# Forming three of four weight sums by adding transfers in a seven-product FFN on one Trainium2 core

## The chip, the cores and the metric

The kernel runs on one core of one Trainium2 chip. The metric is the device time of one execution in microseconds (us), all stages included. Everything is in float32, and every matrix product is made of three passes of TensorE over pairs of rounded parts (below).

## The reference, cut to what matters

Two layers of a diffusion backbone over 640 tokens (512 latent, 128 context). Each layer has an FFN, a token mixer and a second FFN, so there are four FFNs, and these are nearly all of the time:

```
def _swiglu(h, w1, w2):
    gate, up = jnp.split(h @ w1, 2, axis=-1)
    return (jax.nn.silu(gate) * up) @ w2
...
        xp = _half_ffn(xp, m_ctx, 0, norm_pre[i, 0], norm_post[i, 0], ffn_w1[i, 0], ffn_w2[i, 0])
        xs = _half_ffn(xs, m_lat, 0, norm_pre[i, 0], norm_post[i, 0], ffn_w1[i, 0], ffn_w2[i, 0])
```

D_MODEL is 1024, D_FF is 2816, that is 22 f tiles of 128 hidden channels each. For an f tile, `w1` holds a gate block and an up block of 1024 x 128.

## The kernel before, in words

**Products.** A weight tile is 128 x 1024 floats (512 KB) and is called a unit. It is loaded into a `raw` buffer (4 buffers), then split: ScalarE (ACT) writes the rounded part `hi` (line 215), VectorE (DVE) the rest `lo` (line 216); `hi` and `lo` have 6 buffers each (`wts`). TensorE (PE) then makes hi*hi, hi*lo and lo*hi (`mm3`, lines 228 to 230), each matmul with 320 moving columns, half of the tokens.

**Seven block products.** For f tiles 4 to 21 of each FFN (`FAST`) the four block products of the gate and up weights with the two halves of the tokens are made by a scheme of the Strassen-Winograd kind: seven products of 12 matmuls instead of eight. It needs four sums of weight blocks. With g1, g2 the two halves (512 columns each) of the tile's gate unit and u1, u2 those of its up unit, `send` forms g1+u1 (line 179), u1+u2 (line 180, into the up buffer), g1+u1+u2 (line 181) and -(g1+u1+u2)-g2 (line 188, into the gate buffer), all on DVE, 128 x 512 each. The four units of a tile are called `gate`, `sums`, `up` and `all`: the gate unit as loaded, the tile with g1+u1 and g1+u1+u2, the up buffer, and the half formed last. The last two f tiles (`LATE`) make the second token half later, have five products here and, instead of `up` and `all`, a unit `u2`, behind which line 197 forms the last sum for `mix`.

**Order of one f tile** (`w1_fast`): product 1 with `gate`, 2 and 3 with `sums`, 4 with `up`, 5 with `gate`, 6 with `up`, 7 with `all`. The results are taken from PSUM by ACT (lines 687, 698) and DVE (lines 690, 693, 713, 701, 719); PSUM has four `main` and two `score` banks, which go round, so that product 4 of a tile writes the bank that line 701 of the tile before has read.

**Order of the work.** `unit(i, ahead)` sends (loads, sums, splits) all units up to i+ahead when unit i is asked for; that fixes the order in which a scheduler sees them. Each engine and each DMA queue works its own list in order; `high_priority` puts the PSUM work ahead. The sums of a tile stand on DVE some one to two tiles ahead of their product. A `raw` buffer is handed on in the order of release: after line 188 the buffer of a tile's sums takes the up load of the next tile, after the split of the `all` half the buffer of its gate unit takes a later gate load.

**Stages of an FFN** (`plan_ffn`): f tiles 0 to 3 with eight products each, then f4, then a stretch of the second matrix (`w2`, some 28 us of PE), f5 to f8, `w2`, f9 to f12, `w2`, f13 to f16, `w2`, f17 to f21, and the last `w2`. A *run* below is the f tiles between two such stretches: three runs of four tiles, and one of five whose last two are `LATE`. Under the `w2` stretches DVE also makes dot products for the modulation vectors (line 421, 128 loads of 512 KB, most of them in the first three FFNs), with the same `raw` buffers.

**GpSimd (POOL)** has little to do: the power -0.5 of the norms (line 507) and small pieces of the attention.

Of the kernel before, what the change touches and what calls it, by code (L numbers as in the profile page):

```python
# [15 lines left out]
ALU = mybir.AluOpType  # L16
# [94 lines left out]
class Kernel:  # L111
# [54 lines left out]
    def send(self, kind, src):  # L166

        nc, two, one = self.nc, slice(512, UNIT), slice(0, 512)
        at = slice(0, UNIT)
        if kind in ("plain", "block", "gate"):
            raw = self.raw_tile(src)
            self.fast["gate"] = raw
        elif kind == "sums":
            up, gate = self.raw_tile(src), self.fast["gate"]
            raw = self.raw.tile([P, UNIT], F32, tag="raw", name=self.name("sums"))
            nc.vector.tensor_tensor(raw[:, one], gate[:, one], up[:, one], op=ALU.add)
            nc.vector.tensor_tensor(up[:, one], up[:, one], up[:, two], op=ALU.add)  # L180
            nc.vector.tensor_tensor(raw[:, two], gate[:, one], up[:, one], op=ALU.add)  # L181
            self.fast["up"], self.fast["sums"] = up, raw
        elif kind in ("up", "u2"):
            raw = self.fast["up"]
            at = at if kind == "up" else two
        else:
            raw, at = self.fast["gate"], two
            nc.vector.scalar_tensor_tensor(out=raw[:, two], in0=self.fast["sums"][:, two], scalar=-1.0,
                                           in1=raw[:, two], op0=ALU.mult, op1=ALU.subtract)
        n = at.stop - at.start  # L190
        if kind == "block":
            hi, lo = (self.ring(F32R)[:, :n] for _ in range(2))
        else:
            hi, lo = (self.wts.tile([P, UNIT], F32R, tag=tag, name=self.name(tag))[:, :n] for tag in ("hi", "lo"))
        self.split(hi, lo, raw[:, at])
        if kind == "u2":
            nc.vector.scalar_tensor_tensor(out=raw[:, two], in0=self.fast["sums"][:, two], scalar=-1.0,
                                           in1=self.fast["gate"][:, two], op0=ALU.mult, op1=ALU.subtract)
            self.mixed.append(raw)
        return hi, lo  # L200

# [400 lines left out]
    def ffn(self, layer, which, base, boundary):  # L602


        nc = self.nc
        n = layer * 3 + 2 * which
        begun = [False, False]
        g, sums, kept, mixes = {}, {}, {}, {}
        quad = lambda t: t.rearrange("p (c t) -> p c t", c=4)

        def hidden(f, v, half):
            lo, hi = SPAN[half]
            self.hid = self.split(g[f][:, 0, lo:hi], g[f][:, 1, lo:hi], v[:, :HALF])
# [29 lines left out]
        def part(i, k):  # L643
            return sums[i][0][:, k, :], sums[i][1][:, k, :]

        def combine(step):

            if step == 0:
                if n:
                    self.spilled = [self.dram.tile([P, 2 * TOK], F32, tag=f"spill{c}", name=self.name("spill"))  # L650
                                    for c in range(NCH // 2)]
                    for c in range(NCH // 2):
                        nc.sync.dma_start(out=self.spilled[c], in_=self.xs[n][c].rearrange("p c t -> p (c t)"))
                combine.now = {}
            k = step % 2 * 2
            b11, b12, b21, b22 = (self.pair(self.y, c, half) for c in (k, 4 + k) for half in (0, 1))
            if step < 2:
                t = combine.now[k] = [self.temp(("square", "total")[step]).rearrange("p (c t) -> p c t", c=2)
                                      for _ in range(2)]
                steps = ((1, t[0], b12, b11), (2, t[1], b22, t[0]))  # L660
            else:
                t = combine.now[k]
                steps = ((3, t[0], b22, b12), (4, t[1], t[1], b21))
            for i, to, a, b in steps:
                if k == 0:
                    sums[i] = [quad(self.ring(F32R)) for _ in range(2)]
                nc.vector.tensor_tensor(to, a, b, op=ALU.subtract)
                self.split(sums[i][0][:, k : k + 2, :], sums[i][1][:, k : k + 2, :], to)

        high, tt = self.tc.high_priority, nc.vector.tensor_tensor  # L670

        def product(f, ps, unit, at, x, start):
            w = mixes[f] if unit is None else self.unit(base + self.w1_at[f] + unit)
            for k in range(4):
                a = at + k * P
                self.mm3(ps, w[0][:, a : a + P], w[1][:, a : a + P], *x(k), start and k == 0, k == 3, not start)
# [32 lines left out]
        def one(f, a, unit):  # L709
            w = self.bank()[:, :HALF]  # L710
            product(f, w, unit, 0, lambda k: part(1, k), True)
            with high():
                tt(a, a, w, op=ALU.add)
            return w

        def two(f, a, q, w, unit, at):
            product(f, w, unit, at, lambda k: self.h.chunk(4 + k, 1), False)
            with high():
                nc.vector.scalar_tensor_tensor(out=q, in0=w, scalar=-1.0, in1=q, op0=ALU.mult, op1=ALU.subtract)  # L719
                nc.scalar.activation(q, q, AF.Silu)  # L720
                tt(a, a, q, op=ALU.mult)
                hidden(f, a, 1)

        def tail(f):
            a, q = kept[f]
            two(f, a, q, one(f, a, None), None, 512)
# [42 lines left out]
        for op, a, half in self.ffn_plan:  # L769
# [3 lines left out]
            if op == "w1":  # L773
                if not begun[half]:
                    self.finish(half)
                    begun[half] = True
                w1(a, half)
            elif op == "combine":
                combine(a)
            elif op == "fast":  # L780
                w1_fast(a)
            elif op == "mix":
                mixes[a] = self.mix()
            elif op == "tail":
                tail(a)
            elif op == "w2":
                w2(a[0], half, a[1])
                if a[0] < len(SLICES) - 1:
                    passed += 1
                    due = BEHIND[n] * passed // (2 * NCH * (len(SLICES) - 1))  # L790
                    self.behind(due - done)
                    done = due
            elif op == "x":
                self.new_x(n + 1)
                for c in range(NCH // 2):
                    src = self.spilled[c].rearrange("p (c t) -> p c t", c=2) if n else self.io["x"][:, 2 * c : 2 * c + 2, :]
                    nc.sync.dma_start(out=self.xs[n + 1][c], in_=src)
            else:
                boundary(half, acc[half])
# [659 lines left out]
```

## Time and profile before

| | |
|---|---|
| time, median of 3 runs | 2282.19 us (2278.74 to 2282.55) |
| profiled execution | 2277.9 us, span 2276.0 us |
| PE matmul busy | 2241.0 us, 98% of the span |
| DVE busy | 1732.3 us, 76% |
| ACT busy | 1269.3 us, 56% |
| POOL busy | 41.8 us, 2% |
| loads and stores, q1 | 274.63 MB, 36.9% of 16 engines' span |
| granted TensorE clock | 0.997 |

A row of the timeline gives start, duration, engine, line, operation, the tile written and those read, and in brackets how long the engine sat idle before it and on what. A row of the waits gives who waited for whom, the total in us, how often, and the longest. In a row of the windows each engine's busy time stands with its number of instructions. A row of the DMA issues gives the transfer, how often, its size and the median time from issue to landing.

### The profile page before, as it was taken

Reading aid. Unit: us, or ns where it says so; the run is one execution under the profiler, and the core shown is the slowest. Engines: PE = TensorE matmul, PEld = TensorE weight load, DVE = VectorE, ACT = ScalarE, POOL = GpSimd, SP = SyncE. Lnnn points to the kernel's source line nnn. Section 1 sums busy time; section 2 is a strip of 40 time slices with the busy share of each in tenths; the row PEclk is TensorE's granted clock in tenths of the full one; section 3 lists DMA queues with packets and bytes.
Section 4 is the critical chain, followed back from the end, with each engine's and each line's share of the span. In section 5 each row is a group of like instructions: output and inputs, shape, how many; then the busy total and the mean of one; then the engine's idle time right before and its main releaser. Section 6 shows DMA issues by size and latency. Waiting matters only on the chain.

```text
span 2276.0 us, 39329 instructions
## 1 busy us (share of the span) xinstructions
PE 2241.0 (98%) x15680; PEld 2208.5 (97%) x15680; DVE 1732.3 (76%) x3014; ACT 1269.3 (56%) x2460; POOL 41.8 (2%) x64
## 2 busy tenths in 40 slices
PE   7999999999999999999999999999999999999998
PEld 5999999999999999999999999998998999999998
DVE  5889888588788888868878888588677485766674
ACT  4445554565654555556545544577778654545545
POOL 0000000000000000000000000000000000000000
PEclk9999999999999999999999999999999999999999
DMA  8244443334333433443244443424333222332322
GB/s 316 90 133 154 161 130 115 145 97 129 113 112 112 148 120 123 136 160 112 86 128 141 157 130 103 148 92 136 119 111 102 82 72 98 112 93 78 104 88 102
DMA packets 80281, 278.14 MB, mean 122 GB/s; under 512 B 8800, under 2 KB 15200, under 8 KB 79968
## 3 DMA queue, kind: packets, MB, share of 16 engines
q1 hardware_dynamic: 79280, 274.63, 36.9%
q8 instruction: 123, 2.02, 0.4%
q10 hardware_dynamic: 816, 0.98, 0.1%
q14 instruction: 62, 0.51, 0.1%
HBM read 264.04 MB, written 11.53 MB: 121 GB/s over the span
## 4 chain that ended last, share of the span: by engine, by line
PE 92%; DVE 3%; ACT 2%; DMA 2%; issue 0%; DVEq 0%; POOL 0%; SPq 0%; ACTq 0%
PE main L228 27%; PE main L230 26%; PE main L229 26%; PE score L230 3%; PE score L229 3%; PE score L228 3%; PE sum L1286 1%; DMA raw<-in_qkv 1%; DVE lo L216 1%; PE sum L512 1%; PE sum L502 1%; PE score L1219 1%; DMA first<-in_w_mod_k 1%; DVE ring L1065 1%; DVE ring L1077 0%
## 5 line engine op out<-in xcount | busy, mean ns | idle before, releaser
L228 PE MATMUL main<-ring,hi 128*128 128x320 f32 x3872 | 1205.3, 312 | 1.6 <-ACT ring L215 1.6
L229 PE MATMUL main<-ring,hi 128*128 128x320 f32 x3872 | 1197.9, 309 | 1.0 <-DVE ring L216 1.0
L230 PE MATMUL main<-ring,lo 128*128 128x320 f32 x3872 | 1197.4, 309 | 0.0
L228 PEld LDWEIGHTS main<-ring,hi 128*128 128x128 f32 x3872 | 727.8, 188 | 6.2 <-issue 2.7
L229 PEld LDWEIGHTS main<-ring,hi 128*128 128x128 f32 x3872 | 727.9, 188 | 2.0 <-DVE ring L216 1.4
L230 PEld LDWEIGHTS main<-ring,lo 128*128 128x128 f32 x3872 | 727.5, 188 | 0.2 <-issue 0.2
L215 ACT ACTIVATE hi<-raw 128x1024 fp32r<-128x1024 f32 (+1 forms) x366 | 356.1, 974 | 443.5 <-PE main L229 353.6
L216 DVE TENSOR_TENSOR lo<-raw,hi 128x1024 fp32r<-128x1024 f32 (+1 forms) x366 | 408.9, 1118 | 142.2 <-ACT hi L215 140.6
L421 DVE SCALAR_TENSOR_TENSOR junk<-raw,wide 128x1024 bf16<-128x1024 f32 x256 | 312.9, 1222 | 21.0 <-DMA raw<-in_w_mod_t 18.5
L763 ACT ACTIVATE y<-main 128x320 f32<-128x320 f32 x318 | 135.9, 432 | 150.6 <-PE main L230 150.0
L737 ACT ACTIVATE main<-y 128x320 f32<-128x320 f32 x256 | 111.5, 439 | 40.2 <-DVE left L719 27.2
L230 PE MATMUL score<-ring,lo 128*128 128x320 f32 x416 | 128.7, 309 | 0.6 <-DVE lo L216 0.6
L228 PE MATMUL score<-ring,hi 128*128 128x320 f32 x416 | 128.9, 310 | 0.0
L229 PE MATMUL score<-ring,hi 128*128 128x320 f32 x416 | 128.5, 309 | 0.0
L216 DVE TENSOR_TENSOR lo<-sums,hi 128x1024 fp32r<-128x1024 f32 x72 | 88.1, 1223 | 42.6 <-ACT hi L215 42.6
L457 DVE TENSOR_TENSOR total<-total,square 128x640 f32<-128x640 f32 x71 | 58.4, 825 | 80.4 <-ACT square L456 78.6
L215 ACT ACTIVATE hi<-sums 128x1024 fp32r<-128x1024 f32 x72 | 76.3, 1060 | 31.2 <-DVE sums L181 16.8
L228 PE MATMUL main<-ring,ring 128*128 128x320 f32 x288 | 90.9, 316 | 0.0
L230 PE MATMUL main<-ring,ring 128*128 128x320 f32 x288 | 89.1, 310 | 0.0
L229 PE MATMUL main<-ring,ring 128*128 128x320 f32 x288 | 88.9, 309 | 0.0
L230 PEld LDWEIGHTS score<-ring,lo 128*128 128x128 f32 x416 | 78.1, 188 | 0.8 <-DVE lo L216 0.8
L228 PEld LDWEIGHTS score<-ring,hi 128*128 128x128 f32 x416 | 78.1, 188 | 0.0
(211 smaller groups left out, 2599.8 us busy)
## 6 DMA issues: line engine op xcount, KB each, us to landing
raw<-in_w SPq DMA_DIRECT2D x264, 512.0 KB, 3.6
raw<-in_w_mod_t SPq DMA_DIRECT2D x128, 512.0 KB, 4.2
raw<-in_qkv SPq DMA_DIRECT2D x26, 512.0 KB, 3.7
first<-in_w_mod_k SPq DMA_DIRECT2D x16, 512.0 KB, 8.7
spill<-ring SPq DMA_DIRECT2D x12, 640.0 KB, 3.6
ring<-spill SPq DMA_DIRECT2D x12, 640.0 KB, 7.0
raw<-in_bias SPq DMA_DIRECT2D x16, 448.0 KB, 3.3
raw<-in_four_in SPq DMA_DIRECT2D x8, 512.0 KB, 5.8
```

What stands on the lines that cost most here:

```text
L215: a = self.nc.scalar.activation(hi, src, AF.Copy)
L216: return a, self.nc.vector.tensor_tensor(lo, src, hi.bitcast(F32), op=ALU.subtract)
L228: mm(out, whi, xhi, start=start, stop=False)
L229: mm(out, whi, xlo, start=False, stop=False)
L230: self.latest = mm(out, wlo, xhi, start=False, stop=stop)
L421: last = self.nc.vector.scalar_tensor_tensor(out=self.junk, in0=raw, scalar=1.0, in1=self.wide[:, cond, :], op0=ALU.mult, op1=ALU.mult, ac ...
L457: nc.vector.tensor_tensor(acc, acc, sq, op=ALU.add)
L502: self.meant = nc.tensor.matmul(ps[:, j : j + 1], part[:, t : t + P], self.mean, start=i == j == 0 or len(acc) == 1, stop=i == len(acc) - ...
L512: self.spread = nc.tensor.matmul(bank[:, t : t + P], col[:, j : j + 1].to_broadcast([P, P]), self.ident, start=True, stop=True)
L737: nc.scalar.activation(ps[:, :HALF], self.y[:, m, lo:hi], AF.Copy)
L763: nc.scalar.activation(self.y[:, m, lo:hi], ps[:, :HALF], AF.Copy)
L1065: nc.vector.tensor_tensor(ks[p0][rows, KL + to : KL + to + hi - lo], ps[rows, lo - base : hi - base], ks[p0][rows, to : to + hi - lo].bitc ...
```

## The change

What `send` does for `sums` and `all` is changed: of the four sums only g1+u1+u2 is still formed on DVE.

- u1+u2: a transfer from HBM, issued by POOL, adds u2 into the up buffer (line 180 of the new kernel).
- g1+u1: the sums buffer is loaded with g1 by SP (line 179, 256 KB), and a transfer issued by POOL adds u1 to it (line 181).
- the last sum: a transfer issued by POOL adds the tile's g1+u1+u2 from its buffer into the second half of the gate buffer (line 189). A transfer only adds, so the sum has the other sign now, and the lines that use it (in `combine`, `one`, `two`) are changed to match; the instructions there keep their number and shapes.
- behind `u2`, line 197 becomes a plain addition on DVE.
- `product` asks for units four ahead instead of three.

```
             raw = self.raw_tile(src)
-            self.fast["gate"] = raw
+            self.fast["gate"], self.fast["from"] = raw, src
         elif kind == "sums":
             up, gate = self.raw_tile(src), self.fast["gate"]
             raw = self.raw.tile([P, UNIT], F32, tag="raw", name=self.name("sums"))
-            nc.vector.tensor_tensor(raw[:, one], gate[:, one], up[:, one], op=ALU.add)
-            nc.vector.tensor_tensor(up[:, one], up[:, one], up[:, two], op=ALU.add)
+            nc.sync.dma_start(out=raw[:, one], in_=self.fast["from"][:, one])
+            nc.gpsimd.dma_start(out=up[:, one], in_=src[:, two], accum_op=ALU.add)
+            nc.gpsimd.dma_start(out=raw[:, one], in_=src[:, one], accum_op=ALU.add)
             nc.vector.tensor_tensor(raw[:, two], gate[:, one], up[:, one], op=ALU.add)
...
             raw, at = self.fast["gate"], two
-            nc.vector.scalar_tensor_tensor(out=raw[:, two], in0=self.fast["sums"][:, two], scalar=-1.0,
-                                           in1=raw[:, two], op0=ALU.mult, op1=ALU.subtract)
+            nc.gpsimd.dma_start(out=raw[:, two], in_=self.fast["sums"][:, two], accum_op=ALU.add)
...
-            nc.vector.scalar_tensor_tensor(out=raw[:, two], in0=self.fast["sums"][:, two], scalar=-1.0,
-                                           in1=self.fast["gate"][:, two], op0=ALU.mult, op1=ALU.subtract)
+            nc.vector.tensor_tensor(raw[:, two], self.fast["sums"][:, two], self.fast["gate"][:, two], op=ALU.add)
...
-                steps = ((1, t[0], b12, b11), (2, t[1], b22, t[0]))
+                steps = ((1, t[0], b11, b12, ALU.subtract), (2, t[1], b22, t[0], ALU.add))
...
-            w = mixes[f] if unit is None else self.unit(base + self.w1_at[f] + unit)
+            w = mixes[f] if unit is None else self.unit(base + self.w1_at[f] + unit, 4)
...
-                tt(a, a, w, op=ALU.add)
+                tt(a, a, w, op=ALU.subtract)
...
-                nc.vector.scalar_tensor_tensor(out=q, in0=w, scalar=-1.0, in1=q, op0=ALU.mult, op1=ALU.subtract)
+                tt(q, w, q, op=ALU.subtract)
```

From line 189 on the new kernel's line numbers are one lower: the split is at 214 and 215, the PSUM reads of DVE at 689, 692, 712, 700, 718.

**DVE, in the first FFN, while PE makes f6.** `left`, `right` and `main` belong to the PSUM work of f6, `raw` and `sums` to weight buffers; the number tells buffers of one name apart. Before:

```order
L713 TENSOR_TENSOR left_1462<-left_1462,main_1519 128x320
L179 TENSOR_TENSOR sums_1654<-raw_1619,raw_1652 128x512
L180 TENSOR_TENSOR raw_1652<-raw_1652 128x512
L181 TENSOR_TENSOR sums_1654<-raw_1619,raw_1652 128x512
L216 TENSOR_TENSOR lo_1603<-raw_1487,hi_1602 128x512
L701 TENSOR_TENSOR right_1465<-left_1463,main_1468 128x320
L702 TENSOR_TENSOR right_1465<-right_1465,right_1464 128x320
L216 TENSOR_TENSOR lo_1622<-raw_1619,hi_1621 128x1024
```

And now, at the same place:

```order
L712 TENSOR_TENSOR left_1470<-left_1470,main_1533 128x320
L182 TENSOR_TENSOR sums_1631<-raw_1610,raw_1629 128x512
L215 TENSOR_TENSOR lo_1582<-raw_1477,hi_1581 128x512
L700 TENSOR_TENSOR right_1473<-left_1471,main_1476 128x320
L701 TENSOR_TENSOR right_1473<-right_1473,right_1472 128x320
L215 TENSOR_TENSOR lo_1613<-raw_1610,hi_1612 128x1024
```

Of the three sums one is left, at the same place: behind the PSUM read of product 4, ahead of the PSUM read of product 6 (line 701, now 700) and of the split of the next gate unit. It reads the up buffer `raw_1629` that a POOL transfer adds into.

**POOL, the same stretch of the program** (nothing of POOL stood between the norms there before). Its list for f7, f8 and the first tile of the next run:

```order
L180 DMA raw_1496<-in_w 128x512
L181 DMA sums_1498<-in_w 128x512
L189 DMA raw_1477<-sums_1498 128x512
L180 DMA raw_1629<-in_w 128x512
L181 DMA sums_1631<-in_w 128x512
L189 DMA raw_1610<-sums_1631 128x512
```

Three transfers for each f tile, in one list: the one into the up buffer waits for the up load, the one into the gate buffer for the sum on DVE and for the split of the gate unit, which reads what it overwrites.

More of the change, by code (lines that the diff above doesn't have):

```diff
@@ L659, in combine @@
                                       for _ in range(2)]
-                steps = ((1, t[0], b12, b11), (2, t[1], b22, t[0]))
+                steps = ((1, t[0], b11, b12, ALU.subtract), (2, t[1], b22, t[0], ALU.add))
             else:
                 t = combine.now[k]
-                steps = ((3, t[0], b22, b12), (4, t[1], t[1], b21))
-            for i, to, a, b in steps:
+                steps = ((3, t[0], b22, b12, ALU.subtract), (4, t[1], t[1], b21, ALU.subtract))
+            for i, to, a, b, op in steps:
                 if k == 0:
                     sums[i] = [quad(self.ring(F32R)) for _ in range(2)]
-                nc.vector.tensor_tensor(to, a, b, op=ALU.subtract)
+                nc.vector.tensor_tensor(to, a, b, op=op)
                 self.split(sums[i][0][:, k : k + 2, :], sums[i][1][:, k : k + 2, :], to)
```

## The prediction

> **What bounds the kernel now.** I read the page first, then the engines by stretch, then who PE waits for.
>
> ```profile
> span 2276.0 us, 39329 instructions
> PE 2241.0 (98%) x15680; PEld 2208.5 (97%) x15680; DVE 1732.3 (76%) x3014; ACT 1269.3 (56%) x2460; POOL 41.8 (2%) x64
> ```
>
> The windows of three f tiles of the second FFN and of the `w2` stretch behind them (length, then PE, weight loads, DVE, ACT, POOL, clock, DMA share, GB/s):
>
> ```profile
> 728.85:741.17 12.32, 12.32 (x86) 12.32 (x85) 10.59 (x18) 5.92 (x10) 0.00 (x0) 1.00 0.27 84
> 741.17:753.49 12.32, 12.32 (x86) 12.32 (x85) 8.69 (x15) 5.92 (x10) 0.00 (x0) 1.00 0.47 146
> 765.81:793.97 28.16, 28.16 (x194) 28.16 (x193) 26.08 (x42) 16.49 (x35) 0.00 (x0) 1.00 0.47 150
> ```
>
> PE has no gap in these stretches, at full clock, while DVE is busy 10.6 of 12.3 us and 26.1 of 28.2. DVE is the second most loaded engine, but it doesn't set the pace. First PE instructions of product 2 (the only ones into `score`) of two tiles that follow each other:
>
> ```profile
> 742.93 0.31 PE L228 MATMUL score<-ring,hi 128*128 128x320 f32 x1
> 755.25 0.31 PE L228 MATMUL score<-ring,hi 128*128 128x320 f32 x1
> ```
>
> A tile takes 755.25 - 742.93 = 12.32 us for 84 matmuls, 0.1467 each, 1.76 for a product; it starts one product earlier, at 741.17. What PE waited for on DVE's splits, in the whole execution:
>
> ```profile
> PE score L229 <- DVE lo L216: 1.4, 2, 1.3
> PE main L229 <- DVE ring L216: 1.0, 1, 1.0
> PE score L230 <- DVE lo L216: 0.6, 1, 0.6
> ```
>
> That is 3.0 us in all, 0.13% of the span. So the bound is PE's own rate, and a lighter DVE can't bring more than about 3 us here.
>
> **What the change removes.** Duration of each group: least, median, most, in ns.
>
> ```profile
> L179 DVE TENSOR_TENSOR sums<-raw,raw x72: 684/686/700, 56.0 to 2193.8; 128x512 f32<-128x512 f32 x72
> L180 DVE TENSOR_TENSOR raw<-raw x72: 684/691/698, 58.9 to 2194.8; 128x512 f32<-128x512 f32 x72
> L188 DVE SCALAR_TENSOR_TENSOR raw<-sums,raw x64: 684/691/695, 82.2 to 2172.9; 128x512 f32<-128x512 f32 x64
> ```
>
> 72 x 0.686 + 72 x 0.691 + 64 x 0.691 = 143 us of DVE, some 2.1 us of each tile. PE waits for none of it, so on the path it is worth 0, at most the 3.0 us above. The turned signs and line 197 keep their instructions: 0.
>
> **What it adds.** 72 loads of 256 KB on SP and 72 + 72 + 64 = 208 adding transfers of 256 KB on POOL's queue. DMA issues, with the median from issue to landing:
>
> ```profile
> raw<-in_w SPq DMA_DIRECT2D x264, 512.0 KB, 3.6
> first<-in_w_mod_k SPq DMA_DIRECT2D x16, 512.0 KB, 8.7
> ring<-spill SPq DMA_DIRECT2D x12, 640.0 KB, 7.0
> x_out<-ring SPq DMA_DIRECT2D x7, 320.0 KB, 2.5
> k_out<-rms SPq DMA_DIRECT2D x8, 64.0 KB, 1.5
> sk<-in_conds SPq DMA_DIRECT2D x1, 8.0 KB, 2.1
> q1 hardware_dynamic: 79280, 274.63, 36.9%
> ```
>
> Bytes: 72 x 3 x 256 KB from HBM and 64 x 256 KB inside SBUF are 73 MB; at 36.9% for 274.63 MB that is 10 points more, 47% of the DMA engines. Not a bound; it lies beside PE.
>
> What counts is latency. No row shows a transfer that adds. Call A1 the time from issue to landing of the one from HBM into the up buffer, A3 of the one from the sums buffer into the gate buffer. From 8 KB in 2.1 to 512 KB in 3.6 is 1.5 us for 504 KB, so 256 KB lands in 2.85. An adding transfer has to read its destination too: 0.75 more, 3.6. I add 0.4 for an issue by software, which no row gives: A1 = 4.0. A3: 2.5 for 320 KB out of SBUF, 0.2 less for 256 KB, the second read and the issue as above: 3.4. Bounds: 2.1 and 1.5 below (the smallest transfers), 8.7 and 7.0 above (loads that queue). I take the middle since the 512 KB load moves as many bytes and is unqueued. The Trainium skill, "DMA: Bandwidth & Descriptors", section "Anatomy of one DMA — SWDGE (gpsimd) path", gives a transfer issued by GpSimd 2.0 us and its bytes over 436 GB/s, so 2.6 us for 256 KB; no row can show it, and by it the sum below comes out at nothing (first rival).
>
> **The new loop.** DVE while PE makes f6 (728.85 on) and f7 (741.17 on) of the second FFN, the place of the order above; two loads stand below:
>
> ```profile
> 736.47 0.48 DVE L713 TENSOR_TENSOR left<-left,main 128x320 f32<-128x320 f32 x1
> 736.87 0.69 DVE L179 TENSOR_TENSOR sums<-raw,raw 128x512 f32<-128x512 f32 x1
> 737.59 0.69 DVE L180 TENSOR_TENSOR raw<-raw 128x512 f32<-128x512 f32 x1
> 738.31 0.69 DVE L181 TENSOR_TENSOR sums<-raw,raw 128x512 f32<-128x512 f32 x1
> 738.92 0.69 DVE L216 TENSOR_TENSOR lo<-raw,hi 128x512 fp32r<-128x512 f32 x1
> 739.61 0.49 DVE L701 TENSOR_TENSOR right<-left,main 128x320 f32<-128x320 f32 x1
> 740.21 0.49 DVE L702 TENSOR_TENSOR right<-right,right 128x320 f32<-128x320 f32 x1
> 740.62 1.22 DVE L216 TENSOR_TENSOR lo<-raw,hi 128x1024 fp32r<-128x1024 f32 x1
> ...
> 744.09 0.69 DVE L188 SCALAR_TENSOR_TENSOR raw<-sums,raw 128x512 f32<-128x512 f32 x1
> ```
> ```profile
> 744.84 0.33 SPq L157 DMA_DIRECT2D raw<-in_w  x1
> ```
>
> Before, f8's sums are complete at 739.00, 2.2 us before f7 starts, and the up load of the next tile goes out at 744.84, when line 188 (end 744.78) has let go of the sums buffer: 3.7 us into a tile. Now that load waits for the landing of the transfer of line 189, which reads the sums buffer. Line 189 waits on POOL for the sum on DVE and for the split of the gate unit, four DVE instructions later. And the sum waits for the transfer into the up buffer. So each tile hangs on the one before: up load 3.6, A1, sum 0.7, the DVE work to the end of the gate split 740.62 + 1.22 - 738.92 = 2.9, A3, and some 0.1 at each of four handovers (an estimate): 7.6 + 4.0 + 3.4 = 15.0 us against a tile of 12.32. Within a run the sums fall back by 2.7 us per tile.
>
> How far they may fall: behind the sum on DVE stand a split (0.69) and the PSUM read of product 6 (0.49), which product 4 of the next tile waits for, 3 x 1.76 = 5.28 us into it. So the sum may end up to 5.28 - 0.69 - 0.49 = 4.1 us after that tile's start; now it ends 2.2 before. The cover is 6.3 us. Behind the sum, DVE's whole list waits, ACT's next splits with it.
>
> Within a run: the first tile's sums are formed under `w2`. For the third tile the up load goes out 3.7 us into the first, so its sum ends at 3.7 + 3.6 + A1 + 0.7 + 0.2 = 12.2, 0.1 before the second tile starts. Fourth tile: 2.6 after the third starts. Fifth: 5.3, past the limit by 1.2. Only the long run has a fifth, once in each FFN: 4 x 1.2 = 4.8 us.
>
> In the first FFN two runs start late, since the dot products on DVE (line 421) hold up the sums. Last sum of the second tile, and product 2 of the first:
>
> ```profile
> 288.61 0.31 PE L228 MATMUL score<-ring,hi 128*128 128x320 f32 x1
> 366.05 0.31 PE L228 MATMUL score<-ring,hi 128*128 128x320 f32 x1
> ```
> ```profile
> 289.58 0.69 DVE L181 TENSOR_TENSOR sums<-raw,raw 128x512 f32<-128x512 f32 x1
> 365.99 0.69 DVE L181 TENSOR_TENSOR sums<-raw,raw 128x512 f32<-128x512 f32 x1
> ```
>
> They end 3.4 us (290.27 against 286.85) and 2.4 us (366.68 against 364.29) into the run. With line 189 behind them the next up load goes out at 3.4 + 0.1 + A3 + 0.1 = 7.0 and 6.0 instead of 3.7, so the fourth tile's sum ends at 2.6 + 3.3 = 5.9 and 2.6 + 2.3 = 4.9: stalls of 1.8 and 0.8; and in the long one the fifth is 2.7 past the limit instead of 1.2. That is 1.8 + 0.8 + 1.5 = 4.1 us.
>
> Units four ahead: the `hi` split of a unit waits for a `wts` buffer that PE lets go of, which a longer list does not hasten.
>
> ```profile
> ACT hi L215 <- PE main L229: 366.2, 191, 8.1
> ```
>
> Worth 0 beside that wait; where it is short of raw buffers, SP's list only blocks earlier. Below nothing is excluded too, but for the 3.0 us.
>
> Sum: 4.8 + 4.1 = 8.9 us. The profiled execution took 2277.9 (span 2276.0), so 2286.8, say **2287 us**. That execution lies 4.3 below the median of the three runs and 0.8 below the fastest, so a median may come out some 4 higher; the range has room for it.
>
> **The rivals.** 0.2%, 4.6 us, is about what a measurement of this kernel tells from no change.
>
> *The loop fits (not slower).* If A1 + A3 is 6.9 or less, the fifth tile's sum ends within its 4.1 us, and what is left is about 3 us in the first FFN. For it: 3.5 us for the pair by the smallest rows, and landing times of loads include HBM, which the second read doesn't. Against: each of the two must beat a plain 512 KB load. Time 2278, with the median at 2282. The Trainium skill's 2.0 us and bytes over 436 GB/s, from the page named above, would put the pair at 5.2 and decide for this one; the traces bear neither out.
>
> *The transfers are far slower.* With A1 = 7.0 and A3 = 6.4 (queued loads show 8.7 and 7.0) the loop is 21.0 us, 8.7 more than a tile: third sum 2.9 into its tile, fourth 11.6, so 7.5 of stall in each short run and 7.5 + 8.7 = 16.2 in the long one, 4 x (3 x 7.5 + 16.2) = 155 us: 2433. For it: POOL must write what the transfer does while DVE is busy 76% of the span. Against: the 512 KB loads are unqueued at 3.6. At both upper bounds it is some 230 us. The Trainium skill, "SBUF — State Buffer", section "SBUF: two separate sides", tells of a transfer issued by GpSimd that took about 3100 ns beside a DVE copy instead of 620, because DVE held the port through which the descriptors are written; its section "Who interferes with whom" does not count two-input additions that meet a GpSimd write among these. No row here shows it.
>
> *Faster.* The 3.0 us of waits on splits vanish, and the lighter DVE shortens a norm or the attention. Nothing in the waits shows more than that: 2273.
>
> **How the numbers follow.** Forecast (A1 + A3 from 6.9 to 9): 0.41, of which 0.06 lands within 0.2%. The loop fits: 0.39. Far slower: 0.15. Faster: 0.05. The forecast and the fit are close, and the forecast is what the middle values give. So faster 0.05, same 0.06 + 0.39 = 0.45, slower 0.35 + 0.15 = 0.50. At A1 + A3 = 9 (4.9 and 4.1) the loop grows by 4.3 per tile: the short runs stall 1.0, the long one 5.3, 4 x 8.3 = 33, and some 9 more in the first FFN: 2320, on the scale of the median 2324. The range, 2275 to 2335, holds the forecast, the fit and half of the faster case, and leaves out most of the far slower one.
>
> **What would show it.** Right: PE without a gap in the first three tiles of a run and gaps at line 227 behind line 700 in the fifth; DVE idle ahead of line 182 for some 5 us per tile, released by the transfer of line 180; POOL's transfers landing in 3.4 to 4.0 us; DVE busy some 143 us less. The forecast is wrong if the sums of a run don't fall back from tile to tile, if PE's stalls lie under `w2` (ACT waiting for line 181 ahead of the PSUM seeds) or at the norms (line 506 behind a transfer on POOL), or if the two kinds of transfers land in under 3.4 or over 4.5 us.

## The result and the profile after

The changed kernel takes 2474.84 us (median of 4 runs, 2471.95 to 2476.53) against 2281.72 (4 runs of the kernel before beside it): 1.0848 times as long, interval 1.0829 to 1.0866. It lost 193 us where the prediction had 9 and its range ended at 2335. The profiled execution took 2476.53, with a span of 2474.8.

The page's head, for the kernel after:

```profile
span 2474.8 us, 40081 instructions
PE 2303.7 (93%) x15680; PEld 2245.0 (91%) x15680; DVE 1596.7 (65%) x2806; ACT 1253.9 (51%) x2460; POOL 224.2 (9%) x272
```

DVE is lighter by 1732.3 - 1596.7 = 135.6 us, near the 143 that were counted. PE, which had no time to lose, is now idle 7% of the span. Whom its matmuls waited for (us in all, times, longest):

```profile
PE main L227 <- ACT main L736: 45.2, 12, 6.7
PE main L227 <- DVE left L692: 39.9, 34, 3.9
PE main L227 <- ACT left L686: 38.3, 29, 4.4
```

These are reads of PSUM (lines 686, 692) and the seeding of a PSUM bank under `w2` (line 736), 123 us together. What PE lacks is mostly not weights but banks, because DVE and ACT come late to read or fill them. Why they are late stands in their own waits, after:

```profile
DVE sums L182 <- DMA raw<-in_w: 301.7, 64, 8.2
```
```profile
ACT ring L214 <- DVE right L701: 207.3, 52, 8.3
ACT hi L214 <- DMA sums<-in_w: 204.9, 35, 10.0
```

DVE stands 302 us at its sum for the landing of line 180, ACT 205 us at a split for the landing of line 181 and 207 behind DVE. The transfers themselves took what was forecast (KB each, median us from issue to landing):

```profile
sums<-in_w SPq DMA_DIRECT2D x72, 256.0 KB, 3.4
raw<-in_w POOLq DMA_DIRECT2D x72, 256.0 KB, 3.9
sums<-in_w POOLq DMA_DIRECT2D x72, 256.0 KB, 5.1
raw<-sums POOLq DMA_DIRECT2D x64, 256.0 KB, 3.3
```

A1 is 3.9 (forecast 4.0), A3 is 3.3 (forecast 3.4). Line 181, 5.1 us behind a load of 3.4, had been given no price.

**A tile.** Two tiles of the second FFN after (length, then PE, weight loads, DVE, ACT, POOL, clock, DMA share, GB/s), at the place where the tile before took 12.32 without a gap:

```profile
800.57:815.88 15.31, 13.11 (x86) 12.32 (x85) 8.57 (x14) 5.60 (x9) 1.06 (x2) 1.00 0.57 135
815.88:831.20 15.32, 13.15 (x87) 12.37 (x86) 10.65 (x18) 6.13 (x10) 2.59 (x3) 1.00 0.60 137
```

The loop of the prediction is there, at its length. DVE's sum of one tile and of the next (in brackets DVE's idle time before), POOL's issues between them, and SP's up load:

```profile
804.42 0.69 DVE L182 TENSOR_TENSOR sums<-raw,raw 128x512 f32<-128x512 f32 x1 [8.08 <-DMA raw<-in_w]
...
819.70 0.69 DVE L182 TENSOR_TENSOR sums<-raw,raw 128x512 f32<-128x512 f32 x1 [5.96 <-DMA raw<-in_w]
```
```profile
808.26 0.86 POOL L189 DMA_DIRECT2D raw<-sums  x1 [7.49 <-DVE left L718]
815.91 0.86 POOL L180 DMA_DIRECT2D raw<-in_w  x1 [6.79 <-DMA raw<-in_w]
```
```profile
811.58 0.33 SPq L157 DMA_DIRECT2D raw<-in_w  x1
```

From sum to sum 819.70 - 804.42 = 15.28 us: 3.84 to the issue of line 189, 3.3 to the up load (it goes out as that transfer lands), 4.33 to the issue of line 180, 3.79 to the next sum. Forecast: 15.0. What was wrong is how soon it hurts. ACT at that place:

```profile
806.75 0.47 ACT L214 ACTIVATE ring<-right 128x320 fp32r<-128x320 f32 x1 [6.78 <-DVE right L701]
807.12 1.04 ACT L214 ACTIVATE hi<-sums 128x1024 fp32r<-128x1024 f32 x1
808.28 0.47 ACT L719 ACTIVATE left<-left 128x320 f32<-128x320 f32 x1
808.66 0.42 ACT L686 ACTIVATE left<-main 128x320 f32<-128x320 f32 x1
```

DVE's lateness goes over to ACT, whose list holds a split of 1.04 us and two more instructions ahead of line 686. That read ends at 809.08, 8.5 us into the tile, and product 5 wanted its bank after 4 x 1.76 = 7.04. PE's waits in that tile:

```profile
PE main L227 <- DVE left L692: 1.1, 1, 1.1
PE main L227 <- ACT left L686: 0.9, 1, 0.9
PE main L227 <- DVE right L700: 0.2, 1, 0.2
```

The reads by lines 692 and 686 cost it 2.0 us; line 700, the only one that the prediction priced, 0.2. The tile is 3.0 us longer, of which 15.31 - 13.11 = 2.2 is idle time of PE; the rest counts as busy, since at a gap the modelled end of one MATMUL no longer overlaps the next.

**Under `w2`.** ACT after, in the stretch of `w2` behind the same run:

```profile
858.93 1.06 ACT L214 ACTIVATE hi<-sums 128x1024 fp32r<-128x1024 f32 x1 [5.54 <-DMA sums<-in_w]
859.89 0.42 ACT L762 ACTIVATE y<-main 128x320 f32<-128x320 f32 x1
...
861.16 0.43 ACT L736 ACTIVATE main<-y 128x320 f32<-128x320 f32 x1
```
```profile
851.75 0.87 POOL L189 DMA_DIRECT2D raw<-sums  x1 [4.18 <-ACT main L736]
852.38 1.13 POOL L181 DMA_DIRECT2D sums<-in_w  x1
```

Line 181 is issued at 852.38, behind line 189 on POOL's queue, and ACT gets on at 858.93, 6.5 us later. The seed behind it comes at 861.16, and PE waits. It is so in all twelve of PE's waits for line 736: ahead of the seed, ACT stood 3.8 to 10.0 us at the split of a sums unit for line 181. The gap shown (the last column but two is the granted clock):

```profile
859.50:861.64 2.14, 0.00 (x0) 0.00 (x0) 1.62 (x2) 2.14 (x5) 0.00 (x0) 1.00 0.00 0
861.64:866.20 4.56, 4.56 (x20) 4.56 (x21) 3.84 (x7) 3.65 (x9) 0.00 (x0) 0.63 0.83 255
```

After the gap the clock is 0.63 for 4.56 us, which costs 4.56 x 0.37 = 1.7 us on top of the 2.14.

**Where the 193 us lie.** The trace has 80 first MATMULs into `score` (one per fast tile and two more in each FFN). The profiled spans differ by 2474.8 - 2276.0 = 198.8 us. The distances between those matmuls, after less before, sum to 194.0 within the FFNs, 70.2, 44.1, 55.8 and 23.9 in the four FFNs; 122.4 of it between tiles, 71.7 in distances with `w2` in them. Only 4.8 us lie outside. For PE, 136 us of the 198.8 are more idle time (span less busy time, 171.1 against 35.0) and 2303.7 - 2241.0 = 62.7 are more busy time for the same 15680 matmuls. The lower clock behind the gaps is some 48 us of that (an estimate from the mean granted clocks: (1 - 0.978) x 2474.8 - (1 - 0.997) x 2276.0), a quarter of the loss.

### The profile page after: what moved, and what is told of

The parts are those of the page before. It is cut to its first block, busy times and chain, and to the rows that moved or that the text cites. A ratio compares the mean times of both kernels' runs of the same rounds, so it can differ in the third digit from the quotient of the medians.

```text
span 2474.8 us, 40081 instructions
## 1 busy us (share of the span) xinstructions
PE 2303.7 (93%) x15680; PEld 2245.0 (91%) x15680; DVE 1596.7 (65%) x2806; ACT 1253.9 (51%) x2460; POOL 224.2 (9%) x272
## 4 chain that ended last, share of the span: by engine, by line
PE 43%; DMA 28%; DVE 16%; issue 8%; ACT 5%; POOL 1%; DVEq 0%; POOLq 0%; SPq 0%; ACTq 0%
DMA raw<-in_w 14%; PE main L227 12%; PE main L228 12%; PE main L229 12%; DMA sums<-in_w 8%; DVE lo L215 6%; DMA raw<-in_w_mod_t 4%; ACT hi L214 2%; DVE junk L420 2%; DVE ring L215 1%; PE score L228 1%; PE score L227 1%; PE score L229 1%; ACT ring L214 1%; DMA raw<-sums 1%
## 5 line engine op out<-in xcount | busy, mean ns | idle before, releaser
L227 PE MATMUL main<-ring,hi 128*128 128x320 f32 x3872 | 1231.5, 318 | 138.5 <-ACT main L736 45.2
L228 PE MATMUL main<-ring,hi 128*128 128x320 f32 x3872 | 1212.3, 313 | 1.4 <-DVE ring L215 1.3
L229 PE MATMUL main<-ring,lo 128*128 128x320 f32 x3872 | 1210.8, 313 | 0.0
L227 PEld LDWEIGHTS main<-ring,hi 128*128 128x128 f32 x3872 | 741.1, 191 | 168.9 <-DVE left L692 49.1
L228 PEld LDWEIGHTS main<-ring,hi 128*128 128x128 f32 x3872 | 742.0, 192 | 2.7 <-DVE ring L215 2.1
L229 PEld LDWEIGHTS main<-ring,lo 128*128 128x128 f32 x3872 | 740.7, 191 | 0.2 <-issue 0.2
L182 DVE TENSOR_TENSOR sums<-raw,raw 128x512 f32<-128x512 f32 x72 | 49.9, 693 | 315.6 <-DMA raw<-in_w 301.7
L214 ACT ACTIVATE ring<-right 128x320 fp32r<-128x320 f32 x104 | 48.0, 468 | 230.5 <-DVE right L701 207.3
L180 POOL DMA_DIRECT2D raw<-in_w x72 | 63.1, 876 | 996.9 <-DMA raw<-in_w 302.2
L227 PE MATMUL main<-ring,ring 128*128 128x320 f32 x288 | 90.9, 316 | 0.0
L228 PE MATMUL main<-ring,ring 128*128 128x320 f32 x288 | 89.1, 309 | 0.0
```

Source lines behind the costliest of these rows:

```text
L180: nc.gpsimd.dma_start(out=up[:, one], in_=src[:, two], accum_op=ALU.add)
L214: a = self.nc.scalar.activation(hi, src, AF.Copy)
L227: mm(out, whi, xhi, start=start, stop=False)
L228: mm(out, whi, xlo, start=False, stop=False)
L229: self.latest = mm(out, wlo, xhi, start=False, stop=stop)
```

## The experiments

Theories. *Loop:* the tile's chain through the raw buffers is 15.3 us, and everything follows from it. *Lists:* DVE and ACT work through lists in order, a consumer of a transfer stands in them where the operand has not landed, and PSUM reads stand behind it. *Transfers:* their bytes, their issues on POOL or their own slowness. "Loss" is the median less that of the kernel before in the same call.

### One part at a time

Lines 180 and 189 back on DVE, so that only g1+u1 is a transfer:

```diff
-            nc.gpsimd.dma_start(out=up[:, one], in_=src[:, two], accum_op=ALU.add)
+            nc.vector.tensor_tensor(up[:, one], up[:, one], up[:, two], op=ALU.add)
...
-            nc.gpsimd.dma_start(out=raw[:, two], in_=self.fast["sums"][:, two], accum_op=ALU.add)
+            nc.vector.tensor_tensor(raw[:, two], self.fast["sums"][:, two], raw[:, two], op=ALU.add)
```

> Only the sum g1+u1 is formed by a transfer (lines 179 and 181); the other two are back on DVE, with the new signs. The loop theory (each up load hangs on the last sum's transfer, which hangs on DVE's sum, which hangs on the adding transfer into the up buffer: 15.3 us per tile against 12.32) expects no loss, 2282 within 5 us, since both links of the loop that are transfers are gone. The rival theory (ACT waits in order for the landing of line 181, and PSUM reads and seeds stand behind it) expects that a large part of the loss stays, 2330 to 2420, with ACT hi<-sums waiting on the transfer for over 100 us and PE behind lines 686, 692 and 736.

Only line 180 a transfer (lines 179, 181 and 189 on DVE):

> Only u1+u2 is formed by a transfer (line 180); it waits on POOL until DVE has read the up buffer for g1+u1. The loop theory: without the last sum's transfer the up load again goes out about 3.7 us into a tile, lands 3.7 later, the DVE sum takes 0.7, the issue 0.65, the transfer 3.7: the sum on DVE begins about 12.5 us in, at the start of the next tile, and does not fall back further: 2282 to 2305. The ACT theory expects 2282, as nothing that ACT waits for is a transfer of line 181.

Only line 189 a transfer:

> Only the last sum (line 189) is a transfer. The loop theory: the up load waits for it, so a tile's chain is 3.7 (load) + 2.1 (three DVE sums less the one that overlaps) + 2.9 + 0.65 + 3.3 = 12.6 us, 0.3 over a tile: 2282 to 2300. The ACT theory expects 2282.

Lines 180 and 189 transfers, g1+u1 on DVE behind line 182:

```diff
+            nc.vector.tensor_tensor(raw[:, one], raw[:, two], up[:, two], op=ALU.subtract)
```

> u1+u2 and the last sum stay transfers, g1+u1 is formed on DVE from the finished sums (g1 + (u1+u2) - u2, another rounding), so nothing waits for line 181. The loop theory: the loop stays, 0.7 us longer by the DVE instruction, so the loss stays: 2430 to 2500. The ACT theory: the loss goes, 2282 to 2310.

| as transfers | median us | ratio, 95% interval | loss us |
|---|---|---|---|
| g1+u1 | 2384.59 | 1.0435 to 1.0479 | 104.0 |
| u1+u2 | 2379.99 | 1.0418 to 1.0449 | 99.4 |
| last sum | 2287.59 | 1.0018 to 1.0042 | 7.0 |
| u1+u2 and last | 2405.26 | 1.0529 to 1.0561 | 124.6 |

Neither theory comes out as its expectation had it. With g1+u1 alone the loop through line 189 is gone, and 104 us are lost. With u1+u2 alone line 181 is gone, and 99 us are lost where both theories had at most 25. The waits of ACT in the first kernel and of DVE in the second (line 181 there is DVE's sum):

```profile
ACT hi L214 <- DMA sums<-in_w: 257.4, 62, 8.7
```
```profile
DVE sums L181 <- DMA raw<-in_w: 218.9, 66, 5.4
```

Yet neither kernel is free of a loop. The buffer of a tile's sums is let go by the split of the sums unit too, not by the last sum alone, and that split comes late in both. Two up loads of the second FFN that follow each other, with ACT's part of that split between them, in the kernel with g1+u1 alone:

```profile
928.36 0.33 SPq L157 DMA_DIRECT2D raw<-in_w  x1
940.95 1.06 ACT L214 ACTIVATE hi<-sums 128x1024 fp32r<-128x1024 f32 x1 [4.11 <-DMA sums<-in_w]
943.29 0.33 SPq L157 DMA_DIRECT2D raw<-in_w  x1
```

The two are 14.93 us apart, and the second goes out 0.03 us after DVE's part of the split has ended, at 943.26. The split had waited 4.1 us for line 181. With u1+u2 alone, two up loads at about the same place:

```profile
929.64 0.33 SPq L157 DMA_DIRECT2D raw<-in_w  x1
942.92 0.33 SPq L157 DMA_DIRECT2D raw<-in_w  x1
```

Here it is 13.28 us, still over the 12.32 of a tile; the transfer of that kernel takes 5.3 us in the median, where its expectation had 3.7. So these two kernels do not separate the waits in the lists from a loop through the raw buffers: each has both. The last sum as a transfer costs next to nothing alone: 1.6 of its 7.0 us lie in the FFNs.

### Four ahead, or fewer

All sums on DVE, four ahead kept:

> No sum is formed by a transfer: all three are back on DVE. What stays of the change is the turned signs and the units asked for four ahead. The prediction's term of 0 for both expects 2282 within 5 us. A theory that the four ahead itself moves splits in front of PSUM reads and costs time expects 2300 or more.

```diff
-            w = mixes[f] if unit is None else self.unit(base + self.w1_at[f] + unit, 4)
+            w = mixes[f] if unit is None else self.unit(base + self.w1_at[f] + unit)
```

> All of the change but the four ahead: units are asked for three ahead, so DVE's sum and the splits stand one unit later in DVE's and ACT's lists. The theory of the blocked lists (DVE stands at its sum for the landing of line 180, ACT at its split for the landing of line 181, with PSUM reads behind them, and what counts is how late in the lists they stand) expects a good part of the loss gone: each run of tiles gains one unit's time of cover, some 3 us in each of 16 runs and as much under w2: 2370 to 2430. The loop alone (15.3 us per tile, whatever the lists) expects 2455 to 2480.

> All of the change, but units are asked for two ahead, so the sum and the splits stand two units later in the lists than in the changed kernel. Blocked lists: 2310 to 2390, unless PE then waits for weights. Loop alone: 2455 to 2480.

> Lines 179 to 181 are transfers, the last sum is back on DVE (no loop), units are asked for two ahead. Blocked lists and loop together: the up load goes out about 3.7 us into a tile, lands 3.7 later, issue 0.65, transfer 3.7 to 5, so the operands are there 12 to 13 us in, and with the sum placed two units later DVE and ACT hardly wait: 2282 to 2305. If the loss came from anything else in the transfers (their bytes, POOL's issues, HBM traffic) it stays: 2380 or more.

| kernel | median us | ratio, 95% interval | loss us |
|---|---|---|---|
| no transfers, four ahead | 2286.48 | 1.0014 to 1.0037 | 5.6 |
| all, three ahead | 2474.65 | 1.0840 to 1.0872 | 193.8 |
| all, two ahead | 2477.50 | 1.0848 to 1.0891 | 196.6 |
| all but the last sum, two ahead | 2423.69 | 1.0610 to 1.0642 | 142.8 |

The four ahead and the turned signs cost nothing in the FFNs (the distances between tiles are those of before; the 5.6 us lie outside them), as forecast. My expectation for three and two ahead was wrong: nothing moved. So the last kernel, whose 2424 us falls under "2380 or more", does not speak for another cause in the transfers either: its sums did not come later, as its expectation took for granted. The order of DVE's list shows why: the framework's scheduler orders each engine's list itself. Whether units are asked for four, three or two ahead, the same 30 of the 72 sums stand ahead of a read by line 700, with no other of these reads between.

### Consumers later in the lists

So the order was forced (below, the *late* order, against the *planned* one of the kernel after): line 182 and the splits of the sums unit and of the last unit are queued behind the PSUM reads (and seeds) traced before them; three ahead.

```diff
+            with self.behind_of(*self.mark.values()):
-            nc.vector.tensor_tensor(raw[:, two], gate[:, one], up[:, one], op=ALU.add)
+                nc.vector.tensor_tensor(raw[:, two], gate[:, one], up[:, one], op=ALU.add)
...
-                nc.scalar.activation(a, x, AF.Copy)
+                self.mark["act"] = nc.scalar.activation(a, x, AF.Copy)
...
-                tt(a, q, z, op=ALU.subtract)
+                self.mark["dve"] = tt(a, q, z, op=ALU.subtract)
```

> All four transfers of the change stay; units are asked for three ahead, and DVE's sum (line 182) and the splits of the sums unit and of the last one are held in DVE's and ACT's lists behind the PSUM reads traced before them (the sum behind line 692 of the tile before, the split behind its line 686). Blocked lists (DVE and ACT stand at the consumer of a transfer that has not landed, with PSUM reads queued behind it): the loss mostly goes, 2285 to 2340, since a landing 4 us later no longer stands in front of those reads; DVE's wait at the sum falls from 302 us to under 100. Loop alone, or slowness of the transfers themselves: the sums come no faster, 2400 to 2480.

> As the kernel with the late use, but with the last sum back on DVE, so that the loop has one transfer less. Blocked lists: 2282 to 2310, a little under the kernel with all four transfers. If the loop through the last sum is what is left there, the difference between the two is that rest; if it isn't, the two are equal.

> Control: the same order of the lists as in the kernel with the late use, but all three sums on DVE and no adding transfer. It prices the order itself: 2282 to 2295 if the splits still come in time for PE; more if PE then waits for weights, which would have to be taken off the two kernels above.

> The order of the lists of the kernel with the late use, but only u1+u2 is a transfer (line 180); g1+u1 is taken on DVE from the finished sums (g1 + (u1+u2) - u2, another rounding), the last sum on DVE. Compare with only u1+u2 by a transfer in the planned order (2380). If the price is that DVE stands at its sum ahead of PSUM reads, the late order takes most of it away: 2282 to 2310. If the price is in the transfer itself (the up buffer held longer, loads behind it), it stays: 2360 to 2400.

> The late order with u1+u2 and the last sum as transfers and g1+u1 on DVE from the finished sums: the loop is whole, line 181 is gone. If what is left in the kernel with the late use (2434) is ACT's wait for line 181, this falls to 2285 to 2320. If it is the loop, it stays at 2390 to 2440.

Line 189 queued behind line 181 on POOL, in the kernel with all four transfers:

```diff
-            nc.gpsimd.dma_start(out=raw[:, one], in_=src[:, one], accum_op=ALU.add)
+            self.added = nc.gpsimd.dma_start(out=raw[:, one], in_=src[:, one], accum_op=ALU.add)
...
+            with self.behind_of(self.added):
```

> The kernel with the late use, with line 181 always ahead of line 189 of the same tile on POOL. Under w2 POOL's list has them the other way round, so line 181 waits there for DVE's sum, and ACT for line 181 with PSUM reads and seeds behind it. If that order is a large part of the rest, 2360 to 2410, with the loss under w2 halved from 85 us; if line 181 is late for its own sake, 2425 to 2440.

| transfers, late order | median us | ratio, 95% interval | loss us | loss in the planned order |
|---|---|---|---|---|
| none | 2281.19 | 0.9995 to 1.0014 | 1.1 | |
| u1+u2 | 2330.88 | 1.0196 to 1.0230 | 48.2 | 99.4 |
| u1+u2 and last | 2373.89 | 1.0387 to 1.0418 | 91.2 | 124.6 |
| all but last | 2391.55 | 1.0437 to 1.0508 | 111.5 | 142.8 |
| all | 2433.98 | 1.0662 to 1.0693 | 153.9 | 193.1 |
| all, line 181 ahead of 189 | 2441.49 | 1.0687 to 1.0719 | 158.8 | |

The order of the lists is worth 31 to 51 us in each pair, and costs nothing without transfers, so blocked lists are part of the loss. (Two pairs differ in more: "all but last" was asked for two ahead in the planned order, and "u1+u2" takes g1+u1 from the finished sums in the late order, so that its transfer need not wait for that sum, and lands in 3.8 us instead of 5.3.) They are not most of it, 39 of the 193 us for the whole change, and the expectations of 2285 to 2340 for all four, 2282 to 2310 for "all but last" and for "u1+u2", and 2285 to 2320 for "u1+u2 and last" were all too low. DVE's wait at the sum fell (line 185 is that sum here), and ACT's at the split grew:

```profile
DVE sums L185 <- DMA raw<-in_w: 85.7, 42, 5.0
```
```profile
ACT hi L218 <- DMA sums<-in_w: 336.4, 58, 10.9
```

Between tiles the loss fell from 122 to 56 us; in the distances with `w2` it rose from 72 to 85. A sum moved behind one read stands ahead of the next: 48 of the 72 now stand ahead of the read by line 717 (712 before). POOL's order of lines 181 and 189 brought nothing: with `w2` the loss fell from 85 to 73 us, between tiles it rose from 56 to 84. That leaves an earlier start of the operands, and SP's queue shows what holds their loads, in the kernel after:

```profile
SPq L157 <- DMA raw<-sums: 502.5, 55, 31.1
```

55 loads wait for the transfer of the last sum, which reads the buffer that they go to. In the kernel before, loads waited there for line 188 on DVE, 31 times and 4.9 us at most:

```profile
SPq L157 <- DVE raw L188: 135.8, 31, 4.9
```

There are four raw buffers, and a tile takes three.

### More raw buffers

`NRAW`, the number of raw buffers, 4 to 5, with `NBLK`, that of the large buffers named `ring`, 20 to 19 to make room (and 6 with 18). Without transfers, as a control:

> Control for the two kernels with five raw buffers (and 19 blocks instead of 20, to make room): all sums on DVE, three ahead. 2282 to 2300 if one block less costs little; what it costs is to be taken off the other two.

The whole change, its planned order, four ahead:

> The whole change, four ahead, with five raw buffers instead of four: up loads no longer hang on the buffer that the last sum's transfer reads, so the loop opens. If the loop through that buffer is the bulk of the loss, it goes: 2300 to 2380. If DVE and ACT stand at consumers that the planned order puts right behind the transfers wherever these are, it stays: 2420 to 2475.

> Five raw buffers and the late order together: transfers go out earlier and their consumers stand later. Blocked lists expect the loss to shrink most of all kernels with the four transfers: 2300 to 2380, with ACT's wait for line 181's transfer (336 us with four buffers) under 200. If neither lead nor order is what is missing, 2420 to 2440 as with four buffers.

> The whole change in its planned order, four ahead, with six raw buffers and 18 blocks (four buffers: 193 us lost, five: 65, of which 54 in the two FFNs that load most of the modulation weights beside the tiles). If the loss is lead that the raw buffers don't give, the rest falls again: 2282 to 2320. If the rest with five buffers is the transfers' own (their bytes, POOL's issues, the landing times themselves), it stays: 2335 to 2355. One block less may cost something of its own; with 19 blocks it cost 1.4 us.

| kernel | median us | ratio, 95% interval | loss us | of it in the four FFNs |
|---|---|---|---|---|
| no transfers, five | 2282.51 | 0.9997 to 1.0016 | 1.4 | none |
| whole change, four | 2474.84 | 1.0829 to 1.0866 | 193.1 | 70.2, 44.1, 55.8, 23.9 |
| whole change, five | 2345.81 | 1.0264 to 1.0305 | 64.7 | 26.4, 1.1, 28.0, 5.0 |
| five, late order | 2339.64 | 1.0243 to 1.0273 | 58.6 | 24.5, 7.3, 20.1, 7.7 |
| whole change, six | 2304.33 | 1.0082 to 1.0116 | 23.8 | 4.0, 1.2, 5.4, 0.5 |

One buffer takes two thirds of the loss away, in the planned order, a second most of the rest; with five the late order is worth at most some 6 us (the intervals overlap) instead of 39. A tile and the `w2` stretch of the second FFN with five buffers:

```profile
760.86:773.18 12.32, 12.32 (x86) 12.32 (x85) 8.75 (x15) 5.78 (x10) 2.60 (x3) 1.00 0.64 156
785.50:825.98 40.48, 40.48 (x278) 40.48 (x277) 32.53 (x56) 23.54 (x47) 6.12 (x7) 1.00 0.78 214
```

PE is back at 12.32 and 40.48 with the same transfers, at a higher DMA share (0.64 and 0.78 against 0.57) and with more bytes per second (156 to 214 GB/s; before, 84 to 150 in such stretches). So bytes, POOL's issues and contention are not what costs time in this FFN. In the first and the third, which keep 26.4 and 28.0 us, the sixth buffer takes away most of the rest with the same transfers, which speaks against them there too. With six buffers DVE and PE wait as follows:

```profile
DVE sums L182 <- DMA raw<-in_w: 163.2, 56, 7.4
```
```profile
PE main L227 <- DVE left L692: 8.0, 7, 1.7
```

DVE still stands 163 us at its sum, and PE loses 8 us by line 692 instead of 39.9: a wait of DVE for a transfer costs little as long as its operands come early enough against PE. Of the 2302.5 - 2276.0 = 26.5 us by which the profiled spans differ, 11.0 lie in the FFNs; 8.0 are added ahead of the fourth FFN (412.1 us between the tiles around it against 404.1), where two blocks fewer may tell; a control with six buffers wasn't run.

## Why the prediction was wrong

- **The bound, and the worth of the lighter DVE: right.** 135.6 us of DVE bought nothing: even with the loss nearly gone (six buffers, 2304.33) no kernel with the change beats the one before.
- **The sizes of the transfers and the loop: right, in part by luck.** 3.9 and 3.3 against 4.0 and 3.4; 15.28 against 15.0. The parts were not: a plain load of 256 KB took 3.4 in this kernel (2.7 with g1+u1 alone), not 2.85, so that what the adding cost over it is 0.5 and not 1.15. No run shows the 0.4 for an issue by software by itself; what the loop above shows is that POOL began the issue of line 180 0.67 us after the load had landed, where the sum had 0.1 for a handover.
- **"The cover is 6.3 us": the step that failed.** It had two ends, and both were off. The start: the prediction let the first tiles' sums be formed under `w2` at no cost, with the third tile's sum ending 0.1 before the second tile starts. In the run shown, the second tile's sum was already late:

```profile
789.51 0.69 DVE L182 TENSOR_TENSOR sums<-raw,raw 128x512 f32<-128x512 f32 x1 [4.42 <-DMA raw<-in_w]
```
```profile
790.01 0.31 PE L227 MATMUL score<-ring,hi 128*128 128x320 f32 x1
...
802.33 0.31 PE L227 MATMUL score<-ring,hi 128*128 128x320 f32 x1
```

  A tile starts 1.76 before its first MATMUL into `score`, the first tile of this run at 788.25 and the second at 800.57. So the second tile's sum ends (790.20) 2.0 us into the first tile. In the kernel before, it ended at 713.94, 2.6 ahead of the first tile (718.29 - 1.76 = 716.53):

```profile
713.25 0.69 DVE L181 TENSOR_TENSOR sums<-raw,raw 128x512 f32<-128x512 f32 x1
```
```profile
718.29 0.31 PE L228 MATMUL score<-ring,hi 128*128 128x320 f32 x1
```

  After, that is 4.6 us later, and the third tile's sum ends (805.11) 4.5 into the second, not 0.1 ahead. The limit: only line 700 for product 4 was counted, 4.1 us. Line 686 for product 5 and line 692 for product 6 stand behind more work in both lists. The fourth FFN shows it most plainly: the third tile's sum ended there at 2109.87, a microsecond ahead of the second tile (2112.67 - 1.76 = 2110.91), and PE still stalled in that tile, because ACT stood at the split that needs line 181, and DVE at its own part of that split, with line 692 behind it:

```profile
2109.18 0.69 DVE L182 TENSOR_TENSOR sums<-raw,raw 128x512 f32<-128x512 f32 x1 [2.48 <-issue]
```
```profile
2112.67 0.31 PE L227 MATMUL score<-ring,hi 128*128 128x320 f32 x1
```
```profile
2116.02 1.06 ACT L214 ACTIVATE hi<-sums 128x1024 fp32r<-128x1024 f32 x1 [4.04 <-DMA sums<-in_w]
2116.98 0.46 ACT L719 ACTIVATE left<-left 128x320 f32<-128x320 f32 x1
2117.34 0.42 ACT L686 ACTIVATE left<-main 128x320 f32<-128x320 f32 x1
```
```profile
PE main L227 <- DVE left L692: 0.9, 1, 0.9
```

  So the loss is not in the fifth tile of the long run alone: the third tile loses 1.5 to 4.5 us in each of the 16 runs, the second 0.7 to 3.1 in 15 of them, and the fourth of the long ones 5.4 to 6.5. In the first FFN, where two late starts were priced at 4.1 us, the first tile of every run loses 4.4 to 6.2 as well.
- **Line 181: left out of the sum.** The prediction named ACT's wait for it ahead of the seeds as something that would prove it wrong, and gave it no time. As the only transfer it costs 104 us, by the waits and by the loop that it makes together, and under `w2` it is behind all of the 45 us at line 736.
- **The buffers: seen, and stopped short.** The prediction had the up load waiting for the last sum's transfer but counted it only inside a run. It had no term for a chain that starts late after `w2`, nor for a buffer that the split of the sums unit holds, by which the chain is too long (14.9 and 13.3 us) with g1+u1 or u1+u2 as the only transfer. Five and six buffers show that the lack of buffers is the bulk of the loss.
- **The clock: not counted.** The mean is 0.978 against 0.997. Of the 62.7 us more of busy time of PE, some 48 are the slower stretches behind gaps (the estimate above); the rest is put down to matmuls that no longer overlap at a gap.
- **The four ahead: 0, right.** *The rival of far slower transfers* gave 2433, the nearest time, for a reason that isn't there: A1 and A3 were at the forecast's values, and the start and the limit, not the latency, were what it lacked too.
- **Open.** Why the first and the third FFN keep 26.4 and 28.0 us with five buffers and the second only 1.1. Over half of it (13.0 and 17.3) is lost in the first tiles of the runs, right behind a `w2` stretch. They have 36 and 32 pieces of the modulation work behind them, the second 28, the fourth 8, which doesn't order them so; a sixth buffer takes most of it away. Open too is why u1+u2 as the only transfer took 5.3 us, and 3.9 among the others.

## What to carry to other kernels

A transfer that takes an operation's place is priced by the time from when its buffer comes free to when its consumer may go on, on every list in which the consumer stands. With four buffers for three per tile, transfers of 3.3 to 5.1 us in that chain cost 193 us, though DVE, ACT and POOL had room; one buffer more gave 128 back. Price each consumer's list by itself (here ACT's split as much as DVE's sum), find the earliest read queued behind it, and take the start of a run from the stretch ahead of it, not from the steady tiles.

## What the runs showed of the hardware

- A gap of PE of 2.14 us was enough for the granted clock to average 0.63 over the next 4.56 us; the two gaps of about 1 us in a tile (0.9 and 1.1 at lines 686 and 692) left it at 1.00. Of the gaps of PE in that trace, all 18 of 2.1 us or more (the wait at its very start apart) were followed by a mean of 0.50 to 0.69 over the next 4.56 us, and 57 of the 62 between 0.8 and 2.0 us by 1.00. The Trainium skill, "TensorE: Matmul & The Clock Gate", section "Part 1: The HAM clock gate", has the clock halve after an idle window of about 3.4 us and come back after as long a busy one; the way back agrees with the 4.56 us, the way down came sooner here.
- 256 KB that add into SBUF took 3.3 us from SBUF and 3.9 from HBM, a plain load of that size 3.4. That of line 181 took 5.1 in the median: 5.4 for the 46 issued within 1.6 us of the one before, 4.1 for the other 26, and 6.5 where three transfers overlapped. As the only kind of a kernel, that of line 181 took 4.5 and that of line 180 5.3, so the order on the queue is not all of it. The Trainium skill, "DMA: Bandwidth & Descriptors", section "Anatomy of one DMA — SWDGE (gpsimd) path", would give 2.6 (an estimate of the prediction by that page); no kind of them came down to that. An issue held POOL for 0.87 us in the median, and where it waited for a load it mostly began 0.67 us after the landing (815.24 and 815.91 in the loop above).
